# Column sums by token begun in the first expert stage, weight splits traced ahead and a double norm in two independent chains, in a two-block transformer kernel

## The chip, the cores and the metric

The kernel runs on one core of a Trainium2 chip. The time is the device time of one launch, in microseconds (us), from the start of the program to its end on that core. In the core, TensorE (PE in the profile; PEld is its weight loads) does the matmuls and writes to PSUM, VectorE (DVE) and ScalarE (ACT) read and write PSUM and SBUF, and SyncE (SP) issues the loads of the weights. Each engine works through its own list of instructions in the order in which they stand there, and semaphores tie the lists together.

## The reference

Everything is float32, with 256 tokens of 1024 features. A first block (two layers with FFNs) ends in a norm with a gain; a second block has two layers, each with two streams of tokens: x, the first block's output, and ctx.

```python
def rmsnorm(x, g):
    y = x * lax.rsqrt(jnp.mean(x * x, axis=-1, keepdims=True) + EPS)
    return y * g                                   # EPS = 1e-6
...
return rmsnorm(x, final_norm)                      # end of the first block
...
def rms_norm(x):
    return x * lax.rsqrt(jnp.mean(x * x, axis=-1, keepdims=True) + EPS)
def modulate_2(x, shift, scale):
    return rms_norm(x) * (1 + scale) + shift
```

In each layer of the second block a mixer takes `modulate_2` of both streams, and an expert layer (expert choice: 16 experts, each picks 32 tokens) follows and adds its result to them. In layer 0 x is thus normed twice in a row: with the gain of the first block's end, and again without one for the mixer. In layer 1 both streams are normed right after the expert layer of layer 0 has added its result.

## The kernel before

The streams stay in SBUF with features on partitions: `xT` and `xcT` are [128, 8, 256], feature k*128+p of token t at [p, k, t].

**Matmuls.** The second block's projections use three matmuls in a reduced float32 format for each product (`mm3`, L322 to L324): both operands are split into a high and a low part, and high*high, high*low and low*high are summed. A weight slice is split by ScalarE (`wsh`, L314) and VectorE (`wsl`, L315) into one of two buffers; an activation is split when it is made (`hh`, `hl`). So a split can begin only when TensorE has finished with the slice two before it.

**Weights.** SP loads weights in slots of 2 MB (`raw`, L294) that are handed round as a ring: a load waits until whatever was in its slot has been read. The loads that matter here: `ada` (the matrices of scale and shift), `wqk`, `wvf` and `wu` (projections of the mixer) and `sm` (small parameters, among them the one that `kr`, L1343, is multiplied by).

**A norm.** `sums` (L615 to L621): ScalarE squares a 128x256 slice, TensorE adds it over the partitions with a 128x32 weight of ones (L617), eight times; VectorE transposes in blocks of 32 (L619), and a small matmul (L621) leaves the 256 sums as a 128x8 column tile. `inv_sqrt` (L627, then L596 to L606) is ten small VectorE instructions; `spread` (L637, L639) copies and transposes the result to a row for each partition. `modulated` (L664 to L666) then makes the eight slices of `hh` and `hl`, with VectorE, ScalarE and VectorE in turn. For ctx in layer 1 its slices are queued (`later`) and given out between other work.

**The order of the work.** A string, `PLAN`, lists the stages of each layer's mixer (`x` norms a stream, `t` is the projection with `wqk`, `n` its small norms and transposes (L1337 to L1360), `v` that with `wvf`, `u` that with `wu`, `F` takes in loads of `ada` and adds their products, L473 and L479). The program is written in that order, and a scheduler then reorders the instructions of each engine by its own model of when each is ready.

**The double norm** of layer 0 (`st_x`, L1583 to L1592): with s1 the sum of squares of x and s2 that of gain*x, r1 = rsqrt(s1/n + EPS) and r2 = r1*rsqrt(r1*r1*s2/n + EPS). r2 is needed by the mixer's first norm, r1 only for the new x (L1592).

**End of the expert stage.** The last expert product of layer 0 (L1875) is weighted and split (L1884, L1885), put back by token by matmuls (L1888, L1889) and added to `xT` and `xcT` one slice at a time (L1891). Then comes the mixer of layer 1.

## Time and profile before

| | |
|---|---|
| median of three runs | 1552.39 us (1551.93 to 1553.54) |
| the profiled execution | 1550.65 us, of which its span is 1548.9 |
| TensorE busy | 1425.8 us, 92% of the span |
| TensorE weight loads busy | 990.0 us, 64% |
| VectorE, ScalarE busy | 894.8 us, 578.5 us |
| mean granted clock of TensorE | 0.975 of 2.4 GHz |

The profile shows one execution. The span runs from the first to the last instruction that it records; 1.75 us of the time lie around it. Times in rows are us from the span's start, "x8" counts instructions, "out<-in" are the program's names without buffer numbers, and brackets hold how long the engine sat idle before and what ended that. Ends of matmuls are modelled, so the distance between starts says more than a duration. A matmul in full float32 is recorded as two instructions.

In time the kernel is the first block (to 699), the mixer of layer 0 (its first norm and its `wqk`, `wu` and `wvf` projections lie in 699 to 750), its expert layer (to 1196), the mixer of layer 1, and the last expert layer (from about 1290 to the end).

### The profile page before, as it was taken

The page shows a single profiled execution, that of the slowest core. Times are in us where ns is not written, and L with a number is a line of the kernel's source. Part 1 is how long each engine was busy: PE and PEld are TensorE (multiplying, and loading weights), DVE is VectorE, ACT ScalarE, POOL GpSimd, SP SyncE. Part 2 cuts the span into 40 slices and gives each one's busy share as a digit, 9 for nine tenths or more (in the row PEclk, how much of TensorE's full clock was granted, in tenths as well). Part 3 has the DMA queues.
Part 4 walks back from the last instruction along what each step waited for, and adds up shares of the span by engine and source line. Part 5 has one row for each costly group of instructions (what it writes and reads, how often), then busy time and mean ns, then how long its engine had stood idle before and what let it go on. Part 6 is the DMA issues. An engine that isn't in the chain of part 4 may idle for free.

```text
span 1548.9 us, 25284 instructions
## 1 busy us (share of the span) xinstructions
PE 1425.8 (92%) x10360; PEld 990.0 (64%) x10362; DVE 894.8 (58%) x2051; ACT 578.5 (37%) x1180; POOL 5.0 (0%) x15
## 2 busy tenths in 40 slices
PE   5999999999999999999999999999998889897665
PEld 2965899997967999996754784443433656632111
DVE  5668788896776998966665542322224765422011
ACT  3455444443555444544654441211102564310000
POOL 0000000000000000000000000000000000000000
PEclk9999999999999999999999999999999999999788
DMA  9647678597424866554286976899993225699998
GB/s 396 261 178 297 261 275 323 216 394 302 179 110 162 313 259 233 210 210 171 113 315 252 404 305 251 329 414 388 415 368 162 110 109 198 276 428 428 427 427 341
DMA packets 33666, 434.09 MB, mean 280 GB/s; under 512 B 3728, under 2 KB 4368, under 8 KB 6032
## 3 DMA queue, kind: packets, MB, share of 16 engines
q1 hardware_dynamic: 32400, 429.92, 69.8%
q10 hardware_dynamic: 1152, 2.57, 0.5%
q8 instruction: 81, 1.33, 0.3%
q14 instruction: 33, 0.27, 0.0%
HBM read 431.43 MB, written 1.05 MB: 279 GB/s over the span
## 4 chain that ended last, share of the span: by engine, by line
PE 75%; DMA 10%; DVE 9%; ACT 2%; issue 1%; POOLq 0%; DVEq 0%; ACTq 0%; SPq 0%
PE g L322 13%; PE g L324 13%; PE g L323 13%; PE g L1838 7%; PE y L1875 5%; DMA raw<-in_md_dram 4%; PE t L473 3%; DMA raw<-in_mgu_dram 3%; DMA h<-in_mgu_dram 3%; DVE wsl L315 2%; PE m L1838 2%; PE t L1797 2%; PE y L1506 1%; PE g L1523 1%; PE y L1504 1%
## 5 line engine op out<-in xcount | busy, mean ns | idle before, releaser
L314 ACT ACTIVATE wsh<-raw 128x1024 fp32r<-128x1024 f32 (+4 forms) x236 | 242.8, 1033 | 316.4 <-PE g L323 233.9
L315 DVE TENSOR_TENSOR wsl<-raw,wsh 128x1024 fp32r<-128x1024 f32 (+4 forms) x236 | 279.5, 1188 | 88.9 <-ACT wsh L314 88.2
L322 PE MATMUL g<-h,wsh 128*128 128x256 f32 x1072 | 303.8, 286 | 3.7 <-ACT h L657 2.4
L324 PE MATMUL g<-h,wsl 128*128 128x256 f32 x1072 | 304.1, 285 | 2.0 <-DVE wsl L315 2.0
L323 PE MATMUL g<-h,wsh 128*128 128x256 f32 x1072 | 303.9, 285 | 0.2
L322 PEld LDWEIGHTS g<-h,wsh 128*128 128x128 f32 x1072 | 205.1, 192 | 9.5 <-ACT h L665 3.2
L324 PEld LDWEIGHTS g<-h,wsl 128*128 128x128 f32 x1072 | 205.6, 192 | 3.9 <-DVE wsl L315 2.8
L323 PEld LDWEIGHTS g<-h,wsh 128*128 128x128 f32 x1072 | 205.9, 192 | 1.4 <-DVE h L666 0.6
L1838 PE MATMUL g<-raw,xs 128*32 128x512 f32 x1232 | 165.2, 626 | 20.4 <-DMA raw<-in_mgu_dram 19.8
L1875 PE MATMUL y<-raw,a 128*32 128x512 f32 x736 | 99.9, 631 | 9.3 <-DMA raw<-in_md_dram 8.4
L1838 PEld LDWEIGHTS g<-raw,xs 128*32 128x32 f32 x1232 | 38.8, 112 | 106.6 <-issue 70.4
L324 PE MATMUL g<-gh,wsl 128*128 128x256 f32 x352 | 99.8, 284 | 1.5 <-DVE wsl L315 1.5
L322 PE MATMUL g<-gh,wsh 128*128 128x256 f32 x352 | 100.1, 284 | 0.0
L323 PE MATMUL g<-gl,wsh 128*128 128x256 f32 x352 | 99.8, 283 | 0.0
L438 DVE CUSTOM_DVE_ANT_0 raw<-raw,crowc,cols 128x1024 f32<-128x1024 f32 x64 | 80.7, 1280 | 1.2 <-DMA raw<-in_mod1t_dram 1.1
L473 PE MATMUL t<-raw,zc 128*32 128x512 f32 x512 | 71.4, 611 | 6.9 <-DMA raw<-in_mod_dram 6.9
L1802 ACT ACTIVATE xs<-t,modada,ra 128x128 f32<-128x128 f32 x32 | 14.6, 457 | 151.3 <-PE t L1797 107.7
L324 PEld LDWEIGHTS g<-gh,wsl 128*128 128x128 f32 x352 | 67.5, 192 | 1.9 <-DVE wsl L315 1.9
L322 PEld LDWEIGHTS g<-gh,wsh 128*128 128x128 f32 x352 | 67.5, 192 | 1.6 <-issue 1.2
L323 PEld LDWEIGHTS g<-gl,wsh 128*128 128x128 f32 x352 | 67.5, 192 | 0.8 <-issue 0.8
L1875 PEld LDWEIGHTS y<-raw,a 128*32 128x32 f32 x736 | 23.7, 113 | 64.3 <-issue 42.6
L1800 DVE TENSOR_SCALAR xs<-t,ra,modada 128x128 f32<-128x128 f32 x32 | 13.1, 410 | 87.6 <-PE t L1797 50.4
(480 smaller groups left out, 2327.3 us busy)
## 6 DMA issues: line engine op xcount, KB each, us to landing
raw<-in_mgu_dram SPq DMA_DIRECT2D x61, 2048.0 KB, 13.7
raw<-in_md_dram SPq DMA_DIRECT2D x28, 2048.0 KB, 12.0
raw<-in_ffgu_dram SPq DMA_DIRECT2D x22, 2048.0 KB, 8.9
raw<-in_ada_dram SPq DMA_DIRECT2D x19, 2048.0 KB, 7.8
raw<-in_mod_dram SPq DMA_DIRECT2D x12, 2048.0 KB, 9.5
raw<-in_mod1t_dram SPq DMA_DIRECT2D x11, 2048.0 KB, 9.7
raw<-in_ffd_dram SPq DMA_DIRECT2D x16, 1408.0 KB, 7.1
raw<-in_win_dram SPq DMA_DIRECT2D x6, 2048.0 KB, 12.6
```

The lines of the kernel that those rows point to most:

```text
L314: self.nc.scalar.activation(hi, src, AF.Copy)
L315: self.nc.vector.tensor_tensor(lo, src, hi.bitcast(F32), op=ALU.subtract)
L322: mm(out, ah, bh, start=first, stop=False)
L323: mm(out, ah, bl, start=False, stop=False)
L324: mm(out, al, bh, start=False, stop=last)
L438: nc.vector.tensor_tensor_reduce(junk, w[:, q, :], zr[:, i, :], 0.5, self.cols[:, o + 4 * s + q:o + 4 * s + q + 1], ALU.mult, ALU.add, m[: ...
L473: nc.tensor.matmul(acc[32 * j:32 * j + 32, :], zw[:, k, :], w[:, k, :], start=(k < 4), stop=(k >= 4))
L1504: nc.tensor.matmul(sc, self.qT[:, hd, ts], self.kT[:, hd, :nk], start=True, stop=False)
L1506: nc.tensor.matmul(sc, self.qrT[s2, hd // 2, ts], self.krT[s2, hd // 2, :nk], start=False, stop=True)
L1797: nc.tensor.matmul(ps, s["ht"][:, t, k * 128:(k + 1) * 128], oh[:, t, :], start=(t == 0), stop=(t == 1))
L1838: nc.tensor.matmul(banks[si][u][32 * e:32 * e + 32, :], xs[:, k, e * 32:e * 32 + 32], raw[:, u * 2048 + e * 512:u * 2048 + e * 512 + 512], ...
L1875: nc.tensor.matmul(ys[si][32 * e:32 * e + 32, :], hts[si][:, f * 128 + 32 * e:f * 128 + 32 * e + 32], raw[:, (fj * 4 + e) * 512:(fj * 4 + ...
```

## The change

There are three parts. **(1)** The norms of layer 1 begin inside the last write-back of the expert stage, for both streams: `sums2` squares each slice and multiplies it, as a 128x128 weight, with a selector of two columns, so that the sums come out with a token on each partition ([128, 2]), EPS included by one more matmul; `spread2` takes the rsqrt there and makes the row with two matmuls into PSUM. **(2)** The entry `E` at the front of layer 1's plan writes the first two weight splits of `wvf` ahead of the norm; `st_v` picks them up. **(3)** The double norm becomes two chains that don't depend on each other: with `gfin` = sqrt(gain*gain + EPS), made at the start of the kernel by thirteen small VectorE instructions, r2 = rsqrt(sum((x*gfin)^2)/n + EPS*EPS); r1's sum and rsqrt are written after it. The code of an option that was off (`EX`) goes away.

```diff
-PLAN = [..., '+U x0 x1 v0 u0 +H +Q F2 tj nj F1 ...']
+PLAN = [..., 'E +U x0 x1 v0 u0 +H +Q F2 tj nj F1 ...']
...
+    def sums2(self, x):
+        ps = self.ps(self.stag)[:, :2]
+        nk = x.shape[1]
+        nc.tensor.matmul(ps, self.ident, self.epsc, start=True, stop=False)
+        for k in range(nk):
+            sq = self.w([128, 256], "a256", NA2)
+            nc.scalar.activation(sq, x[:, k, :], AF.Square, scale=1.0 / 32)
+            for t in range(2):
+                nc.tensor.matmul(ps, sq[:, t * 128:t * 128 + 128], self.sel2[:, t, :], start=False, stop=(k == nk - 1 and t == 1))
+        return ps
+    def spread2(self, cp):
+        y = self.w([128, 2], "rsy2", 2)
+        self.rsqrt(y, cp, self.w([128, 2], "rst2", 2), self.w([128, 2], "rsc2", 2))
+        r = self.ps("y")[:, :256]
+        for t in range(2):
+            self.nc.tensor.matmul(r[:, t * 128:t * 128 + 128], y[:, t:t + 1].to_broadcast([128, 128]), self.ident, start=True, stop=True)
+        return r
...
-            w = self.split(raw[:, k0 * 512:(k0 + 2) * 512], 1024)
+            w = self.pre.pop(0) if self.pre else self.split(raw[:, k0 * 512:(k0 + 2) * 512], 1024)
...
         if si == 1:
             self.pump(len(self.vq))
-            self.h[1] = self.hc if l == 0 else self.modulated(xc, ..., later=VX > 0)
+            r = self.spread2(self.early.pop(1)) if l else None
+            self.h[1] = self.hc if l == 0 else self.modulated(xc, ..., r=r, later=VX > 0)
         elif l == 1:
-            r = (...) if EX else None
+            r = self.spread2(self.early.pop(0))
             self.h[0] = self.modulated(x, ..., r=r, pair=self.pair2())
         else:
-            y1 = self.inv_sqrt(self.sums(x), 1024)
-            s2 = self.sums(x, gain)
-            v = self.w([128, 8], "rsc2", 1)
-            nc.vector.tensor_tensor(v, y1, y1, op=ALU.mult)
-            nc.vector.tensor_tensor(v, v, s2, op=ALU.mult)
-            y2 = self.inv_sqrt(v, 1024)
-            nc.vector.tensor_tensor(y2, y2, y1, op=ALU.mult)
-            r2 = self.spread(y2)
+            r2 = self.spread(self.inv_sqrt(self.sums(x, self.gfin), 1024, EPS * EPS))
+            s1 = self.sums(x)
             a = self.scale_cols(mn, 1, "final_norm", 0)
             self.h[0] = self.modulated(x, a, mn, 0, 0, r=r2, pair=self.pair2())
-            r1 = self.spread(y1)
+            r1 = self.spread(self.inv_sqrt(s1, 1024))
...
+            elif c == "E":
+                self.pre = [self.split(self.raw("wvf")[:, i * 1024:i * 1024 + 1024], 1024) for i in range(2)]
...
-                    if EX and q == 3 and n == 1 and si == 0:
+                    if q == 3 and n == 1:
                         self.stag = ST[1]
-                        self.rx = ...
+                        self.early[si] = self.sums2(x)
```

With the new lines the line numbers shift. After the change the split stands at L313 and L314, `mm3` at L321 to L323, the products with `ada` at L490, `sums` at L654 to L660, `inv_sqrt` at L666, `spread` at L676 and L678, `modulated` at L703 to L705, the transposes of stage `n` at L1397, the write-back at L1927 and L1928.

VectorE, mixer of layer 0, the end of the norm. Before, the rsqrt of r1 (its last instruction is L606), then the second chain's transpose of its sums (L619), the product with r1 and the second rsqrt:

```order
L606 SCALAR_TENSOR_TENSOR rsy_7935<-rsc_7933,rsy_7935 128x8
L1583 TENSOR_TENSOR rsc_1233_7975<-rsy_7935 128x8
L619 STREAM_TRANSPOSE a_1231_7971<-y_7946 128x256
L1584 TENSOR_TENSOR rsc_1233_7975<-rsc_1233_7975,t_7973 128x8
L627 TENSOR_SCALAR rsc_7978<-rsc_1233_7975 128x8
```

After the change the chain of r2 (from `y_7927`) comes first and ends in its `spread` (L676, L678); L658 is the transpose of the other sums, those of r1 (`y_7973`), and L703 the first instruction of `modulated`:

```order
L623 SCALAR_TENSOR_TENSOR rsy_7958<-rsc_7956,rsy_7958 128x8
L676 COPY a_1228_7969<-rsy_7958 128x256
L678 STREAM_TRANSPOSE rsr_7971<-a_1228_7969 128x256
L658 STREAM_TRANSPOSE a_1239_7998<-y_7973 128x256
L703 SCALAR_TENSOR_TENSOR a_1244_8006<-xT_61,acol_8002,rsr_7971 128x256
L703 SCALAR_TENSOR_TENSOR a_1245_8010<-xT_61,acol_8002,rsr_7971 128x256
```

The second rsqrt has left the way to `modulated`, but the transpose that waits for the other sums still stands ahead of it.

TensorE, the same stage, where the ctx half of `wqk` ends (`g_8047` last) and the x half begins (`g_8048`). Before:

```order
L324 MATMUL g_8047<-wsh_8078,h_7145 128x448
L473 MATMUL t_8167<-raw_1268_8165,zc_1198_7872 32x512 x8
L473 MATMUL t_8179<-raw_1270_8177,zc_1198_7872 32x512
L322 MATMUL g_8048<-wsh_8050,hh_1240_7998 128x448
L323 MATMUL g_8048<-wsl_8051,hh_1240_7998 128x448
```

After; L656 is the last of the column sums of r1, `t_8186` the first product with `ada`:

```order
L656 MATMUL y_7973<-a_1238_7995,ones_68 32x256
L660 MATMUL t_8000<-a_1239_7998,cons_66 128x8
L490 MATMUL t_8186<-raw_1273_8184,zc_1204_7895 32x512
L321 MATMUL g_8067<-wsh_8069,hh_1242_8004 128x448
L322 MATMUL g_8067<-wsl_8070,hh_1242_8004 128x448
```

One product with `ada` stands here now, where nine stood. The others stand at the end of the stage (four in its middle). Before, the end of the `wqk` stage and the start of `wu` (`y_8294`):

```order
L323 MATMUL m_8049<-wsl_8135,hh_1240_7998 128x448
L324 MATMUL m_8049<-wsh_8134,hl_1241_7999 128x448
L473 MATMUL t_8179<-raw_1270_8177,zc_1198_7872 32x512 x3
L322 MATMUL y_8294<-h_7145,wsh_8290 128x256
L323 MATMUL y_8294<-h_7145,wsh_8290 128x256
```

After, the same place (`y_8313` is the start of `wu`):

```order
L322 MATMUL m_8068<-wsl_8154,hh_1242_8004 128x448
L323 MATMUL m_8068<-wsh_8153,hl_1243_8005 128x448
L490 MATMUL t_8186<-raw_1273_8184,zc_1204_7895 32x512 x3
L490 MATMUL t_8198<-raw_1275_8196,zc_1204_7895 32x512 x8
L1397 MATMUL t_8240<-cons_66,a_1287_8237 128x128 x2
L1397 MATMUL t_8251<-cons_66,a_1290_8248 128x128
L1397 MATMUL t_8240<-cons_66,a_1287_8237 128x128
L1397 MATMUL t_8251<-cons_66,a_1290_8248 128x128 x2
L1397 MATMUL t_8288<-cons_66,a_1301_8285 128x128
L1397 MATMUL t_8299<-cons_66,a_1304_8296 128x128
L321 MATMUL y_8313<-h_7168,wsh_8309 128x256
```

The last reads of both `ada` slots (`raw_1273`, `raw_1275`) now come after the whole `wqk` stage, and eight transposes of stage `n` stand ahead of `wu`.

VectorE, start of layer 1's mixer. Before, after the transpose of the sums two weight splits (L315) stand with the rsqrt, whose end is shown here:

```order
L604 SCALAR_TENSOR_TENSOR rsc_11877<-rsc_11877,rst_11880 128x8 x2
L606 SCALAR_TENSOR_TENSOR rsy_11879<-rsc_11877,rsy_11879 128x8
L637 COPY a_1980_11890<-rsy_11879 128x256
L639 STREAM_TRANSPOSE rsr_11892<-a_1980_11890 128x256
L664 SCALAR_TENSOR_TENSOR a_1982_11894<-xT_61,acol_11844,rsr_11892 128x256
```

After; `y_11819` and `y_11873` are the token sums of x and of ctx, `rsy_1991` and `rsy_2006` their rsqrt:

```order
L621 SCALAR_TENSOR_TENSOR rsc_1993_11943<-rsc_1993_11943,rst_1992_11942 128x2 x2
L613 TENSOR_SCALAR rsy_2006_11992<-y_11873 128x2
L623 SCALAR_TENSOR_TENSOR rsy_1991_11941<-rsc_1993_11943,rsy_1991_11941 128x2
L614 TENSOR_SCALAR rsy_2006_11992<-rsy_2006_11992 128x2
L616 TENSOR_TENSOR rst_2007_11993<-rsy_2006_11992 128x2
L617 TENSOR_TENSOR rst_2007_11993<-rst_2007_11993,y_11873 128x2
L314 TENSOR_TENSOR wsl_11931<-raw_1983_11928,wsh_11930 128x1024
L314 TENSOR_TENSOR wsl_11935<-raw_1983_11928,wsh_11934 128x1024
L703 SCALAR_TENSOR_TENSOR a_1998_11960<-xT_61,acol_11956,y_11953 128x256
```

The first instruction of ctx's rsqrt (L613) has come ahead of the last of x's, and both splits ahead of `modulated`. TensorE at the same place, after the change: the last write-backs (`t_11861` and the two after it are those of ctx) with the pairs of column sums (L635) between them:

```order
L635 MATMUL y_11819<-sel_7_72,a_1963_11845 128x2 x2
L1927 MATMUL t_11861<-a_1919_11586,a_1965_11853 128x256
L1928 MATMUL t_11861<-a_1919_11586,a_1966_11854 128x256
L635 MATMUL y_11819<-sel_7_72,a_1964_11849 128x2 x2
L1927 MATMUL t_11865<-a_1919_11586,a_1965_11853 128x256
L1928 MATMUL t_11865<-a_1919_11586,a_1966_11854 128x256
L635 MATMUL y_11873<-sel_7_72,a_1972_11875 128x2 x2
L1927 MATMUL t_11869<-a_1919_11586,a_1965_11853 128x256
```

After these, seven more pairs for `y_11873` and the two matmuls of x's `spread2` stand ahead of the mixer's first matmul. Before the change the eight sums of ctx stood further on, inside the `wvf` stage.

## Rows read from the trace of the kernel before

**Rows 1.** Windows: span, busy time by engine, granted clock, DMA share, GB/s.
```profile
1202.00:1208.00 6.00, 5.67 (x15) 3.95 (x16) 5.77 (x15) 4.17 (x12) 0.00 (x0) 0.63 0.02 4
...
1221.00:1233.00 12.00, 8.61 (x66) 7.98 (x65) 9.64 (x21) 6.99 (x18) 0.00 (x0) 1.00 0.71 282
...
1500.00:1549.00 49.00, 27.87 (x164) 6.84 (x160) 6.09 (x11) 1.19 (x2) 0.00 (x0) 0.85 0.85 358
```

**Rows 2.** Timeline of TensorE from layer 0's norm to the `wvf` stage: start, duration, instruction.
```profile
713.09 2.76 PE L473 MATMUL t<-raw,zc 128*32 128x512 f32 x18
716.33 0.47 PE L322 MATMUL g<-wsh,hh 128*128 128x448 f32 x1 [0.48 <-ACT hh L665]
...
732.59 1.06 PE L473 MATMUL t<-raw,zc 128*32 128x512 f32 x6
733.58 0.39 PE L322 MATMUL y<-h,wsh 128*128 128x256 f32 x1
...
744.21 0.50 PE L323 MATMUL g<-wsl,hh 128*128 128x512 f32 x1
```

**Rows 3.** Timeline of VectorE in the same norm.
```profile
710.92 0.45 DVE L619 STREAM_TRANSPOSE a<-y 128x256 f32<-128x256 f32 x1 [4.13 <-PE y L617]
...
715.25 1.28 DVE L664 SCALAR_TENSOR_TENSOR a<-xT,acol,rsr 128x256 f32<-128x256 f32 x3
...
723.16 1.04 DVE L315 TENSOR_TENSOR wsl<-raw,wsh 128x896 fp32r<-128x896 f32 x1
```

**Rows 4.** Timeline of SP's queue: two loads of this stretch.
```profile
715.07 0.33 SPq L294 DMA_DIRECT2D raw<-in_sm_dram  x1
724.23 0.33 SPq L294 DMA_DIRECT2D raw<-in_wu_dram  x1
```

**Rows 5.** DMA view of 690 to 746: size, us from issue to landing.
```profile
raw<-in_sm_dram SPq DMA_DIRECT2D x1, 2048.0 KB, 8.6
...
raw<-in_wu_dram SPq DMA_DIRECT2D x1, 1024.0 KB, 4.8
```

**Rows 6.** Timeline of VectorE at the start of layer 1's mixer.
```profile
1195.17 0.88 DVE L1891 SCALAR_TENSOR_TENSOR xcT<-t,modada,xcT 128x256 f32<-128x256 f32 x2 [0.50 <-PE t L1889]
...
1201.25 1.28 DVE L664 SCALAR_TENSOR_TENSOR a<-xT,acol,rsr 128x256 f32<-128x256 f32 x3
```

**Rows 7.** Timeline of TensorE there, to the end of the `wvf` stage.
```profile
1190.54 0.64 PE L617 MATMUL y<-a,ones 128*32 128x256 f32 x8
...
1202.34 0.80 PE L322 MATMUL g<-wsh,hh 128*128 128x512 f32 x1 [5.49 <-ACT hh L665]
...
1220.90 0.39 PE L324 MATMUL g<-wsh,hl 128*128 128x512 f32 x1
1221.12 0.28 PE L322 MATMUL y<-hh,wsh 128*128 128x256 f32 x1
```

**Rows 8.** Waits of SP's queue, 1236 to 1300: total, times, longest.
```profile
SPq L294 <- DVE a L1467: 44.2, 1, 44.2
```

**Rows 9.** Windows at the kernel's start; columns as in rows 1.
```profile
14.00:17.00 3.00, 0.11 (x4) 0.00 (x0) 3.00 (x13) 0.60 (x1) 0.00 (x0) 1.00 1.00 426
17.00:19.00 2.00, 1.91 (x16) 0.50 (x16) 1.76 (x11) 0.00 (x0) 0.00 (x0) 1.00 1.03 438
19.00:22.00 3.00, 0.02 (x3) 0.00 (x0) 0.84 (x2) 0.00 (x0) 0.00 (x0) 1.00 0.98 404
22.00:25.00 3.00, 2.77 (x16) 0.90 (x20) 0.00 (x0) 0.00 (x0) 0.00 (x0) 0.50 1.02 423
```

**Rows 10.** Timeline of TensorE: matmuls with a full float32 weight of 128x128.
```profile
944.18 0.71 PE L1797 MATMUL t<-a,h 128*128 128x128 f32 x4
944.73 0.61 PE L1797 MATMUL y<-a,h 128*128 128x128 f32 x4
...
1215.08 0.28 PE L621 MATMUL t<-a,cons 128*128 128x8 f32 x2
1215.22 0.71 PE L322 MATMUL g<-wsh,hh 128*128 128x512 f32 x2
```

More of the change, by code (lines that the diff above doesn't have):

```diff
@@ L34 @@
 VX = 1
-EX = 0
 AD = [int(c, 16) for c in 'A2220']
@@ L357, in setup @@
         nc.vector.memset(self.ones, 1.0)
+        self.epsc = self.t(c, [128, 2], F32, "epsc")
+        nc.vector.memset(self.epsc, EPS)
+        self.sel2 = self.t(c, [128, 2, 2], F32, "sel2")
+        nc.vector.memset(self.sel2, 0.0)
+        for t in range(2):
+            nc.vector.memset(self.sel2[:, t, t:t + 1], 1.0)
+        self.gfin = self.t(c, [128, 8], F32, "gfin")
         self.sel16 = self.t(c, [128, 32], F32, "sel16")
@@ L364, in setup @@
         self.pq, self.pf, self.pn, self.vc, self.pc, self.rowz = [], [], 0, 0, 0, {}
-        self.known = {}
+        self.known, self.early = {}, {}
         self.add_ring(3)
@@ L370, in setup @@
         self.stag = "t"
+        g = self.col("final_norm", 0, 8)
+        t = self.w([128, 8], "acol", 3)
+        nc.vector.tensor_tensor(self.gfin, g, g, op=ALU.mult)
+        nc.vector.tensor_scalar(self.gfin, self.gfin, EPS, None, op0=ALU.add)
+        c = self.w([128, 8], "acol", 3)
+        nc.vector.tensor_copy(c, self.gfin)
+        y = self.w([128, 8], "acol", 3)
+        self.rsqrt(y, c, t, c)
+        nc.vector.tensor_tensor(self.gfin, self.gfin, y, op=ALU.mult)
     def drop(self, *cms):
@@ L591, in scale_cols, with rsqrt @@
         return a
-    def rsqrt(self, y, c, t):
+    def rsqrt(self, y, c, t, u=None):
         nc = self.nc
@@ L606, in rsqrt @@
         nc.vector.scalar_tensor_tensor(y, c, 1.0, y, op0=ALU.add, op1=ALU.mult)
+    def sums2(self, x):
+        nc = self.nc
+        ps = self.ps(self.stag)[:, :2]
[11 more added lines that the diff above has]
+        r = self.ps("y")[:, :256]
+        for t in range(2):
+            self.nc.tensor.matmul(r[:, t * 128:t * 128 + 128], y[:, t:t + 1].to_broadcast([128, 128]), self.ident, start=True, stop=True)
+        return r
     def sums(self, x, gain=None):
@@ L622, in sums, with inv_sqrt @@
         return cp[:, :8]
-    def inv_sqrt(self, cp, n):
+    def inv_sqrt(self, cp, n, eps=EPS):
         nc = self.nc
         c = self.w([128, 8], "rsc", 2)
-        nc.vector.tensor_scalar(c, cp, 1.0 / n, EPS, op0=ALU.mult, op1=ALU.add)
+        nc.vector.tensor_scalar(c, cp, 1.0 / n, eps, op0=ALU.mult, op1=ALU.add)
         y = self.w([128, 8], "rsy", 3)
```

11 lines of the change are left out of this document (5 added, 6 removed).

## The prediction

> **What bounds the kernel now.** I read the windows first, to find where TensorE is not busy, then the timelines of TensorE, VectorE and SP at the two places that the change touches, and last the waits of SP's queue.
>
> TensorE is the bound of most of the kernel. In the norm of layer 0 it has work for the whole stretch: the nine products with `ada` (18 records from 713.09) cover all of its wait for `hh` but 0.48 us [rows 2]. VectorE has the waits there, 4.13 us for the second chain's sums [rows 3]. Whoever removes one of those waits gains only what TensorE waits, and whoever makes TensorE wait here loses it, since no slack follows.
>
> The start of layer 1's mixer is different. The last write-back ends at 1195.17 + 0.88 = 1196.05, `modulated` begins 5.2 us later [rows 6], and TensorE stands for 5.49 us; the `wvf` stage then takes from 1202.34 to 1221.12 [rows 7], the first six microseconds of it at a granted clock of 0.63, and in 1221 to 1233 TensorE is busy for 8.61 of 12 us [rows 1]. So this place has something to give.
>
> The end is bound by loads (DMA share 0.85, TensorE 27.87 of 49 [rows 1]). Whether a shift of the mixer reaches the end is told by SP's queue: the first load of the last experts waits 44.2 us for an instruction of the mixer, a VectorE one at L1467 [rows 8], so what the mixer gains or loses passes on.
>
> **Layer 0, the double norm.** The second chain's way from its sums to `modulated` was 710.92 to 715.25, 4.33 us [rows 3]. It would be gone if r2 could go on alone. But in VectorE's order the transpose of r1's sums stands ahead of the first `modulated`, and those sums now end as the last matmuls ahead of the x half, at about 713.1, where the ctx half ended [rows 2]. With the transpose's 0.45 [rows 3] `modulated` begins at 713.6 in place of 715.25: 1.65 us are won, and the x half starts at 714.7.
>
> Of the nine products one still stands in the wait. Eight go to the end of the `wqk` stage: 16 records at 2.76/18 = 0.153 us, 2.45 us [rows 2]. The stage itself ends at 732.59 - 1.65 = 730.9; three products (0.99, from the distance of two starts [rows 2]) follow until 731.9, then the eight until 734.4. If that were all, `wu` would begin 0.8 us late (before at 733.58).
>
> It is not all, because slots are handed round. `ada`'s slots are now free only at 731.9 and 734.4, so three loads change places: `sm` takes the slot of `wqk`, and waits for its fourth split, 723.16 + 1.04 - 1.65 = 722.6 in place of 715.07 [rows 3, 4]; it lands 8.6 us later [rows 5], at 731.2, and holds up `kr`, which stands on VectorE ahead of the second rsqrt of stage `n`. `wu` takes the slot of the first `ada` and is issued at 731.9 in place of 724.23 [rows 4]; with its 4.8 us [rows 5] it lands at 736.7. The split on ScalarE comes after that, about 1.0 us (the VectorE half of one took 1.04 [rows 3]), and stands behind stage `n`'s copies, which wait for the late rsqrt: `wu`'s matmuls begin at about 738.1. `wvf` is issued at 734.4; at `sm`'s 8.6 it lands at 743.0, while `wu` is still computed.
>
> The `wu` stage lasted 733.58 to 744.21, 10.6 us [rows 2], eight transposes within. These now stand ahead of it, in the wait; at the nearest price, 0.55 for four records of a 128x128 weight [rows 10], they were 1.1 us of it. So the next stage begins at 738.1 + 9.5 = 747.6 in place of 744.21: **+3.4 us**. Low bound +2.5 (ScalarE's queue adds nothing: 737.7, and a `modulated` that starts 0.5 sooner); high bound +5.5, below.
>
> **The clock.** TensorE would stand from 734.4 to 738.1 with only transposes. After 3 us of waiting the granted clock was still 1.00 once (14 to 17, then 17 to 19) and 0.50 once (19 to 22, then 22 to 25) [rows 9]; six microseconds at 0.63 after 5.49 us of waiting cost 0.37 x 6 = 2.2 us [rows 1, 7]. I count no fall in layer 0, and a half in layer 1. The Trainium skill, page TensorE: Matmul & The Clock Gate, section on oscillation in real kernels, says that gaps in the matmul stream send the array back to its half clock, so that the next burst starts cold. Rows 9 agree in one case of two. By that rule layer 0 would pay 1.5 to 2.2 us more, and the sum would be about +0.4 instead of -1.5.
>
> **Layer 1, sums in the write-back.** The trace has no matmul with a full 128x128 weight and two columns. One with eight columns took 0.14 from its start to the next [rows 10]; one with 128 columns 0.55/2 = 0.275 [rows 10]. I take 0.22, nearer to the second, since there too each matmul loads its own weight. The first group is ten matmuls (eight sums and two of EPS), 2.2 us, in place of 0.64 [rows 7]: +1.55. Then a pair stands ahead of each of five write-backs, where three groups stood. What such an interlude costs, changing over included, I work out from the `wvf` stage: 1221.12 - 1202.34 = 18.8 us hold 48 matmuls at 1221.12 - 1220.90 = 0.22 to 0.23 [rows 7], 10.9 us, and 2.2 us of slow clock; the remaining 5.7 are eight sums of ctx, 0.71 each. Three at 0.71 become five at 0.75: +1.6. The write-backs end 3.2 us later, at 1199.25.
>
> Ctx's last square, its pair and the hand-over take another 1.3 us (estimated from two instructions of about 0.4 and their waits), to 1200.55. VectorE then has the first instruction of ctx's rsqrt, and only behind it the last of x's; five such instructions are 1.0 us. The two splits, 1.2 us each (an estimate from 1.04 for 896 columns [rows 3], for 1024), stand ahead of `modulated`, which begins at 1203.95 in place of 1201.25 [rows 6]. So the norm is **later**, by 2.7 us, though its sums began sooner.
>
> What is won is behind it. TensorE starts 1.1 us after `modulated` (1202.34 against 1201.25 [rows 6, 7]), at 1205.05. The stage is now 10.9 us without sums of ctx; I add 1.3 for a third split that waits behind `modulated` on VectorE, or for the rest of a slow clock. It ends at 1217.25 in place of 1221.12: -3.9. Of the 3.4 us of idle time in 1221 to 1233 [rows 1] I give back 1.0, since ctx's chain no longer competes there with splits. **-4.9 us.** Bounds: at 0.275 a matmul, 1.1 more; with the whole slow clock 0.9 more, with a second late split 1.0 more, and nothing given back 1.0: -0.9. At 0.14, 1.6 less, no added 1.3 and a little more given back: -8.
>
> **The start.** `gfin` is 13 small VectorE instructions, 2.2 us at the 0.17 of their kind (17 to 19: 1.76 us for 11 [rows 9]). TensorE waits there for loads (DMA share near 1.0 in 14 to 25 [rows 9]), which hide it; without that cover it would be 2.2 us. The removed products of the second rsqrt lay in VectorE's waiting time. Both: 0.
>
> **Sum.** +3.4 - 4.9 = -1.5 us: 1550.65 of the profiled execution becomes 1549.1. That execution is 1.74 below the median of 1552.39; from the median, 1550.9.
>
> **The rivals.**
> - *Slower: layer 1 gives nothing back.* Its norm waits for ctx's sums and both splits. If a matmul costs 0.275, the clock falls whole and the idle time stays, the gain is 0.9 and the sum +2.5, 1554.9; with layer 0 at its upper end +4.6, 1557.0. It decides by more than 0.2% (3.1 us, about what a measurement of this kernel can tell from no change) when the first `modulated` of layer 1 begins later than about 1207. For it: VectorE's order. Against: ctx's 5.7 us are taken off in any case. 0.18.
> - *The clock falls in layer 0 too*: the sum +0.4, 1552.8. For it rows 9's second case, against it the first. 0.13.
> - *Faster: layer 0 loses nothing.* Loads land sooner than 8.6 and 4.8 in a quieter queue, or the transposes and the `ada` products fill the wait. Then only the 0.8 us of moved products are late, less the 1.1 of transposes that go into the wait: about 0, and layer 1 gives -4.9 or more: 1547.5, down to 1544.4. Against it: `wu`'s slot is free only at 731.9, whatever the queue. 0.22.
> - *No effect*: both places lose and win less than 1 us, 1552.4. 0.05.
> - The forecast keeps 0.42, its own range 1548.5 to 1553.5.
>
> **How the numbers follow.** The range leaves out the far ends of the slower and the faster rival, about 0.1 at each side: 1545.5 to 1556. Faster by over 0.2%: most of the faster rival (0.20) and a third of the forecast (0.14): 0.34. Slower by over 0.2%: two thirds of the slower rival (0.12), a third of the clock's (0.04) and a little of the forecast: 0.18. Within: 0.48.
>
> **What the profile after would show.** Right: `modulated` of layer 0 at about 713.6; `wu` issued near 732 and TensorE idle for 3 us ahead of its first matmul; the next stage at 747.6. In layer 1, write-backs that end near 1202.6 (3.4 late from layer 0, 3.2 by themselves), `modulated` at 1207.4, a `wvf` stage of 12 us without sums, the `wu` stage at 1220.7. Wrong: `wu`'s matmuls in layer 0 at 733 or so (then the slots did not matter); column sums that cost 0.4 us a matmul; or an idle stretch in layer 1 that moves from ahead of the `wvf` stage into it, so that it still ends at 1221 plus what layer 0 lost.

## The result, and the profile after

The changed kernel takes **1563.81 us** (median of five runs, 1562.81 to 1567.59) where the kernel before, run beside it, takes 1552.39 (1550.68 to 1553.71): a ratio of 1.0077, interval 1.0063 to 1.009. It is slower by 11.4 us, above the range. The profiled execution took 1563.81, its span is 1562.0, the mean granted clock 0.970.

Where the time went is read from SP's queue, whose loads follow the work that frees their slots. First four loads of the kernel before (start, duration, instruction): the first `ada` load of layer 0's mixer, the first `md` load of its expert layer, `wqk` of layer 1, and the first load after layer 1's mixer.

```profile
692.88 0.33 SPq L294 DMA_DIRECT2D raw<-in_ada_dram  x1
...
918.44 0.43 SPq L294 DMA_DIRECT2D raw<-in_md_dram  x1
...
1161.21 0.33 SPq L294 DMA_DIRECT2D raw<-in_wqk_dram  x1
...
1289.29 18.55 SPq L294 DMA_DIRECT2D raw<-in_mgu_dram  x4
```

The same loads after the change, with `sm` and `wu` of layer 0 between them:

```profile
693.29 0.33 SPq L293 DMA_DIRECT2D raw<-in_ada_dram  x1
...
722.34 0.33 SPq L293 DMA_DIRECT2D raw<-in_sm_dram  x1
732.32 0.33 SPq L293 DMA_DIRECT2D raw<-in_wu_dram  x1
...
924.52 0.43 SPq L293 DMA_DIRECT2D raw<-in_md_dram  x1
...
1167.78 0.33 SPq L293 DMA_DIRECT2D raw<-in_wqk_dram  x1
...
1304.94 0.33 SPq L293 DMA_DIRECT2D raw<-in_mgu_dram  x1
```

The queue is 0.41 us late ahead of layer 0's mixer, 6.08 behind it, 6.57 ahead of layer 1's mixer and 15.65 behind it. So layer 0 costs 5.7 us, layer 1 9.1, and the end gives about 2.5 back (span 13.1 longer). Below, "shifts +5.7/+9.1" stands for these two differences: from `ada` to `md`, and from `wqk` to the load after the mixer, each against before. They come from one execution each (the first is -0.2 to -0.4 in the kernels whose layer 0 is unchanged); the verdicts rest on the medians.

**Layer 0.** TensorE from the last products with `ada` to `wvf`, in answer to [rows 2]:

```profile
731.21 2.78 PE L490 MATMUL t<-raw,zc 128*32 128x512 f32 x22
...
734.85 0.44 PE L1397 MATMUL t<-cons,a 128*128 128x128 f32 x2 [0.55 <-ACT cq L1399]
...
739.29 0.51 PE L321 MATMUL y<-h,wsh 128*128 128x256 f32 x1 [0.62 <-ACT wsh L313]
...
749.79 0.40 PE L321 MATMUL g<-wsh,hh 128*128 128x512 f32 x1
```

Before the change, the first `wvf` product of layer 0 stands ahead of the one in [rows 2]:

```profile
743.52 0.63 PE L322 MATMUL g<-wsh,hh 128*128 128x512 f32 x2
```

VectorE in the norm, in answer to [rows 3]:

```profile
713.26 0.45 DVE L658 STREAM_TRANSPOSE a<-y 128x256 f32<-128x256 f32 x1 [5.26 <-PE y L656]
713.63 1.24 DVE L703 SCALAR_TENSOR_TENSOR a<-xT,acol,rsr 128x256 f32<-128x256 f32 x3
```

Windows (columns as in [rows 1]):

```profile
736.00:739.00 3.00, 1.20 (x4) 0.44 (x4) 0.00 (x0) 2.94 (x8) 0.00 (x0) 1.00 1.05 407
739.00:742.00 3.00, 2.61 (x11) 2.32 (x12) 2.36 (x2) 1.18 (x2) 0.00 (x0) 0.56 0.83 350
742.00:745.00 3.00, 3.00 (x24) 3.00 (x24) 0.12 (x1) 0.38 (x1) 0.00 (x0) 0.87 0.78 235
```

`modulated` begins earlier, as forecast; `wu` is issued 8.1 us later than before [rows 4], TensorE stands in six pieces, 3.0 us in all, ahead of its first matmul, and then runs at a lower clock until about 743.

**Layer 1.** TensorE, in answer to [rows 7]; L635 are the sums by token, two records for each matmul:

```profile
1197.16 1.93 PE L635 MATMUL y<-sel,a 128*128 128x2 f32 x16
...
1199.49 0.50 PE L635 MATMUL y<-sel,a 128*128 128x2 f32 x4
1199.86 0.37 PE L1927 MATMUL t<-a,a 128*128 128x256 f32 x1
...
1201.44 0.85 PE L635 MATMUL y<-sel,a 128*128 128x2 f32 x4
1202.15 0.56 PE L1927 MATMUL t<-a,a 128*128 128x256 f32 x1
...
1205.28 5.97 PE L635 MATMUL y<-sel,a 128*128 128x2 f32 x28
...
1215.40 0.79 PE L321 MATMUL g<-wsh,hh 128*128 128x512 f32 x1 [2.61 <-ACT hh L704]
...
1224.98 0.50 PE L322 MATMUL g<-wsl,hh 128*128 128x512 f32 x1 [0.94 <-DVE wsl L314]
...
1230.61 0.28 PE L321 MATMUL y<-hh,wsh 128*128 128x256 f32 x1
...
1249.30 0.53 PE L322 MATMUL g<-wsl,h 128*128 128x192 f32 x1 [3.95 <-DVE wsl L314]
```

VectorE, in answer to [rows 6] (L1930 is the write-back's addition):

```profile
1205.52 0.48 DVE L1930 SCALAR_TENSOR_TENSOR xcT<-t,modada,xcT 128x256 f32<-128x256 f32 x1 [0.80 <-PE t L1928]
...
1211.28 0.16 DVE L613 TENSOR_SCALAR rsy<-y 128x2 int32<-128x2 int32 x1 [3.83 <-PE y L635]
1211.36 0.15 DVE L623 SCALAR_TENSOR_TENSOR rsy<-rsc,rsy 128x2 f32<-128x2 f32 x1
...
1214.33 1.26 DVE L703 SCALAR_TENSOR_TENSOR a<-xT,acol,y 128x256 f32<-128x256 f32 x3
...
1247.76 0.48 DVE L703 SCALAR_TENSOR_TENSOR a<-xcT,acol,y 128x256 f32<-128x256 f32 x1
1248.15 1.09 DVE L314 TENSOR_TENSOR wsl<-raw,wsh 128x896 fp32r<-128x896 f32 x1
```

Windows, first the last write-backs of the kernel before:

```profile
1192.00:1198.00 6.00, 3.75 (x20) 1.95 (x19) 4.57 (x10) 2.93 (x5) 0.00 (x0) 1.00 0.00 0
```

After the change:

```profile
1194.00:1200.00 6.00, 5.72 (x49) 4.00 (x42) 2.70 (x7) 2.18 (x4) 0.39 (x1) 1.00 0.13 44
1200.00:1206.00 6.00, 6.00 (x31) 6.00 (x31) 2.60 (x7) 3.42 (x9) 0.00 (x0) 0.52 0.01 3
1206.00:1212.00 6.00, 5.68 (x27) 5.60 (x28) 1.86 (x14) 2.31 (x3) 0.00 (x0) 0.50 0.00 0
...
1248.00:1254.00 6.00, 4.70 (x17) 4.45 (x18) 2.64 (x4) 0.51 (x1) 0.00 (x0) 0.50 0.00 0
```

Three things matter here. A record of the sums takes 0.12 us in the first group and 0.21 in the last; in between, the granted clock goes to half while TensorE is recorded busy for 6.00 of 6.00 us (the longest gap in the records ahead of that is 0.28 us, at 1196.67). VectorE waits 3.83 us for ctx's sums, with the last instruction of x's rsqrt (L623) behind that wait. And at 1249 TensorE waits 3.95 us for a `wsl` that stands on VectorE behind a slice of ctx, and the clock falls again.

### The profile page after: what moved, and what is told of

It reads as the page before. It is cut to its first block, busy times and chain, and to the rows that moved or that the text cites. A ratio compares the mean times of both kernels' runs of the same rounds, so it can differ in the third digit from the quotient of the medians.

```text
span 1562.0 us, 25376 instructions
## 1 busy us (share of the span) xinstructions
PE 1437.6 (92%) x10402; PEld 1005.4 (64%) x10402; DVE 895.1 (57%) x2057; ACT 580.6 (37%) x1180; POOL 5.0 (0%) x15
## 4 chain that ended last, share of the span: by engine, by line
PE 76%; DMA 9%; DVE 8%; ACT 3%; issue 1%; ACTq 0%; DVEq 0%; SPq 0%
PE g L323 13%; PE g L322 13%; PE g L321 13%; PE g L1877 7%; PE y L1914 5%; DMA raw<-in_md_dram 4%; PE t L490 3%; DMA raw<-in_mgu_dram 3%; DMA h<-in_mgu_dram 3%; PE m L1877 2%; DVE wsl L314 2%; PE t L1836 2%; PE y L1545 1%; PE g L1562 1%; PE y L1543 1%
## 5 line engine op out<-in xcount | busy, mean ns | idle before, releaser
L313 ACT ACTIVATE wsh<-raw 128x1024 fp32r<-128x1024 f32 (+4 forms) x236 | 242.6, 1032 | 319.8 <-PE g L322 229.4
L314 DVE TENSOR_TENSOR wsl<-raw,wsh 128x1024 fp32r<-128x1024 f32 (+4 forms) x236 | 279.8, 1190 | 95.7 <-ACT wsh L313 94.7
L321 PE MATMUL g<-h,wsh 128*128 128x256 f32 x1072 | 303.9, 286 | 3.7 <-ACT h L696 2.4
L323 PE MATMUL g<-h,wsl 128*128 128x256 f32 x1072 | 304.3, 285 | 1.9 <-DVE wsl L314 1.9
L321 PEld LDWEIGHTS g<-h,wsh 128*128 128x128 f32 x1072 | 205.2, 192 | 9.5 <-ACT h L704 3.2
L323 PEld LDWEIGHTS g<-h,wsl 128*128 128x128 f32 x1072 | 205.7, 192 | 3.7 <-DVE wsl L314 2.7
L323 PE MATMUL g<-gh,wsl 128*128 128x256 f32 x352 | 99.9, 284 | 1.7 <-DVE wsl L314 1.7
L321 PE MATMUL g<-gh,wsh 128*128 128x256 f32 x352 | 100.1, 284 | 0.0
L490 PE MATMUL t<-raw,zc 128*32 128x512 f32 x512 | 73.3, 627 | 5.1 <-DMA raw<-in_mod_dram 5.1
L323 PEld LDWEIGHTS g<-gh,wsl 128*128 128x128 f32 x352 | 67.5, 192 | 2.3 <-DVE wsl L314 2.3
L321 PEld LDWEIGHTS g<-gh,wsh 128*128 128x128 f32 x352 | 67.5, 192 | 1.6 <-issue 1.2
L1839 DVE TENSOR_SCALAR xs<-t,ra,modada 128x128 f32<-128x128 f32 x32 | 13.1, 410 | 87.6 <-PE t L1836 49.4
```

The source lines that it names most:

```text
L313: self.nc.scalar.activation(hi, src, AF.Copy)
L314: self.nc.vector.tensor_tensor(lo, src, hi.bitcast(F32), op=ALU.subtract)
L321: mm(out, ah, bh, start=first, stop=False)
L323: mm(out, al, bh, start=False, stop=last)
L490: nc.tensor.matmul(acc[32 * j:32 * j + 32, :], zw[:, k, :], w[:, k, :], start=(k < 4), stop=(k >= 4))
```

## The experiments

Eighteen kernels ran. Theory A: the narrow sums bring the clock down. Theory B: the place of the norm and the order that the scheduler makes of it, whatever the clock. Theory C: the late slot of `wu` is the whole loss in layer 0.

**1. The parts apart.** `double_norm_alone` has part (3) only:

```diff
-'E +U x0 x1 v0 u0 ...
+'+U x0 x1 v0 u0 ...
...
-r = self.spread2(self.early.pop(0))
+r = None
...
-if q == 3 and n == 1:
+if False:
```

> Only part 3 is kept (the double norm as two chains); layer 1's mixer begins as before the change. In the changed kernel SP's queue was 0.41 us late before layer 0's norm and 6.08 us late after it. If the loss of layer 0 is part 3's own, through the slots that are freed late, this kernel is 5 to 6.5 us slower than the kernel before, with wu issued near 732 and a granted clock under 1.00 in 736 to 742. The rival, that the loss at layer 0 came from what else is in the program (a later start, other buffers), gives less than 2 us.

1556.93 us against 1552.63, ratio 1.0023 (1.0013 to 1.0032), shifts +5.8/+1.4. By its median it loses 4.3 us, a little under the range. Layer 0's loss comes from part (3) and needs nothing of the others.

`early_sums_alone` has parts (1) and (2), with the double norm as before:

```diff
-r2 = self.spread(self.inv_sqrt(self.sums(x, self.gfin), 1024, EPS * EPS))
-s1 = self.sums(x)
+y1 = self.inv_sqrt(self.sums(x), 1024)
+s2 = self.sums(x, gain)
...
+r2 = self.spread(y2)
...
-r1 = self.spread(self.inv_sqrt(s1, 1024))
+r1 = self.spread(y1)
```

> Only parts 1 and 2 are kept (sums by token in the write-back, splits traced ahead); the double norm is as before the change. SP's queue lost another 9.5 us between 1171 and 1305 in the changed kernel, of which 3 were given back later. First theory, the column sums with two columns bring the clock down while TensorE is busy with them: 6 to 9 us slower than before, granted clock at 0.50 from the write-back on. If the parts add up without touching each other, this run and double_norm_alone together make about 11.4 to 13 us. The rival, that layer 1 lost only because it was reached with the slots and loads of a late layer 0: under 3 us.

1555.91 (ten runs, 1554.82 to 1562.98), 1.0025 (1.0013 to 1.0038), shifts -0.4/+12.3. Slower, and in layer 1 alone, but by its median 3.3 us: between the 6 to 9 of the one theory and the "under 3" of the other. The profiled execution is the longest of the ten; eight lie between 1554.8 and 1556.8, so the +12.3 is likely too large for the usual one. The two parts sum to 7.6 us and the whole change costs 11.4: they don't add.

**2. What in the early sums costs time.** `early_old_sums`: as `early_sums_alone`, but the sums that begin early are the old ones (a 32-column weight of ones, 256 moving columns). The same two lines change for ctx, with `pop(1)`.

```diff
-self.early[si] = self.sums2(x)
+self.early[si] = self.sums(x)
-r = self.spread2(self.early.pop(0))
+r = self.spread(self.inv_sqrt(self.early.pop(0), 1024))
```

> As early_sums_alone, but the sums in the write-back are the old ones (weight of ones with 32 columns, 256 columns moving, VectorE transpose, spread by VectorE), begun at the same place for both streams, with the splits ahead. First theory (narrow matmuls cost the clock): the granted clock stays at 1.00 through the write-back and the sums, the write-backs end about 3 us sooner than in early_sums_alone, and the time is 4 to 9 us under early_sums_alone, at or below the kernel before. The rival (the order on VectorE, with ctx's sums and both splits ahead of the first norm, costs the time): as slow as early_sums_alone within 3 us, at a clock of 1.00.

1546.27, 0.9956 (0.9942 to 0.9971), shifts -0.3/-4.4. The clock is 1.00 through the write-back and the sums, and falls behind them, where TensorE waits for the norm:

```profile
1196.00:1202.00 6.00, 4.73 (x24) 2.06 (x24) 4.51 (x9) 3.49 (x7) 0.00 (x0) 1.00 0.02 4
1202.00:1208.00 6.00, 2.46 (x7) 2.00 (x8) 5.74 (x28) 1.56 (x4) 0.00 (x0) 0.69 0.00 0
```

`wide_selector`: the narrow sums again, but the selector's two columns are repeated 64 times each, so that 128 columns move through the same weight.

```diff
-ps = self.ps(self.stag)[:, :2]
+pf = self.ps(self.stag)[:, :128]
+ps = pf.rearrange("p (t j) -> p t j", j=64)
...
-nc.tensor.matmul(ps, self.ident, self.epsc, start=True, stop=False)
+nc.tensor.matmul(ps, self.ident, self.epsc.unsqueeze(2).to_broadcast([128, 2, 64]), start=True, stop=False)
...
-    nc.tensor.matmul(ps, ..., self.sel2[:, t, :], ...)
+    nc.tensor.matmul(ps, ..., self.sel2[:, t, :].unsqueeze(2).to_broadcast([128, 2, 64]), ...)
-return ps
+return ps[:, :, 0]
```

> As early_sums_alone, but each sum by token has 128 moving columns in place of two (the selector's two columns repeated 64 times; the result is the same and the weights are too). More work for TensorE in each matmul. First theory: the clock stays at 1.00, or falls later, so that a matmul costs at most the 0.275 us of a 128-column one in place of 0.43, and the kernel is 2 to 6 us faster than early_sums_alone though its matmuls are longer. The rival (the loading of 128x128 weights in full float32 sets the pace, and the clock falls for the wait alone): 0 to 3 us slower than early_sums_alone, the clock at 0.50 as there.

1548.04, 0.9969 (0.9956 to 0.9981), shifts -0.2/-0.25: 64 times the columns, and 7.9 us less than `early_sums_alone`. Its TensorE timeline and two windows:

```profile
1195.36 3.06 PE L636 MATMUL y<-sel,a 128*128 128x128 f32 x26
...
1201.23 0.50 PE L321 MATMUL g<-wsh,hh 128*128 128x512 f32 x1 [1.12 <-ACT hh L705]
...
1232.43 0.53 PE L322 MATMUL g<-wsl,h 128*128 128x192 f32 x1 [3.96 <-DVE wsl L314]
```

```profile
1190.00:1196.00 6.00, 6.00 (x55) 6.00 (x55) 3.68 (x10) 5.18 (x12) 0.00 (x0) 1.00 0.10 36
1196.00:1202.00 6.00, 3.87 (x29) 3.42 (x28) 5.59 (x23) 2.30 (x6) 0.00 (x0) 1.00 0.01 1
```

TensorE and its weight loads are as busy as in the changed kernel's 1200:1206, but the clock stays at 1.00; a record takes 0.12 us (3.06 for 26), as with two columns at full clock. Theory A holds for the clock. Theory B may have a share of the time: with the wide form the scheduler no longer puts ctx's first instruction ahead of x's last, so the 7.9 us hold clock and order together. And the 3.96 us wait is still there.

**3. E.** The plan entry taken out, once with narrow and once with old sums:

```diff
-'E +U x0 x1 v0 u0 ...
+'+U x0 x1 v0 u0 ...
```

> As early_sums_alone (3.3 us slower than before by its median, 10.4 in its profiled execution), without the two splits traced ahead. With the old sums the splits ahead were worth 3.7 us. If they help here too, 6 to 8 us slower than before; if what matters is the clock that the narrow sums bring down, within 2 us of early_sums_alone, and its granted clock at 0.50 through the sums.

1558.53, 1.0038 (1.0025 to 1.0051), shifts -0.4/+11.8: 2.6 us more than with E by the medians, but the two intervals overlap.

> As early_old_sums (6.4 us faster than before), without the two splits traced ahead. Before the change the scheduler had moved x's sums into the write-back by itself, and put the two splits between them and the rsqrt. If the gain comes from ctx's sums having left the wvf stage, it stays: 5 to 7 us faster than before. If it comes from the splits, 0 to 2 us faster.

1549.6, 0.9985 (0.9975 to 0.9995), shifts -0.3/-1.5: 3.3 us more than `early_old_sums`, and between the two ranges expected. Part (2) gains about three microseconds with the old sums; with the narrow ones as much is likely, but not shown.

**4. The slot of `wu`.** In layer 0 `wu` gets a buffer of its own (8 KB a partition) in place of a slot of the ring, so it needn't wait for `ada` (the plan also opens and closes the pool of that buffer):

```diff
+if nm == "wu" and self.l == 0:
+    s = self.t(self.wux, [128, 2048], F32, "raww", 1)
+    self.nc.sync.dma_start(s, src)
+    self.raws[nm, i] = s
+else:
     self.raws[nm, i] = self.slot(src)
```

With part (3) alone:

> As double_norm_alone (4.3 us slower than before), but wu of layer 0 is loaded into a buffer of its own, so its load need not wait for the slot of the first ada load. The order of the products with ada (eight at the end of the wqk stage) stays. If the late slot is the cause, wu is issued right behind sm, near 723, its matmuls follow the wqk stage with less than 1 us of idle time, the clock stays at 1.00 there, and the time comes to -1.7 to +0.8 us against before. The rival (kr, the late rsqrt of stage n and the transposes hold up wu's split on ScalarE whatever the load does): +3 to +5 us as without the buffer.

1550.37, 0.9988 (0.9978 to 0.9998), shifts -0.2/0.0, where `double_norm_alone` had 1556.93 and +5.8. In this stretch (705 to 751) TensorE has one idle piece left, and the clock is 1.00:

```profile
711.81 0.39 PE L660 MATMUL t<-a,cons 128*128 128x8 f32 x2 [0.54 <-DVE a L658]
```

With the whole change; here, and in the last kernel of 8, `spread2` also shares the small tiles of the old rsqrt in place of its own:

> The changed kernel with wu of layer 0 in its own buffer; narrow sums and ctx's order stay. double_norm_wu_apart was 6.2 us under double_norm_alone: 1556.5 to 1558.5. If what layer 1 loses depends on how layer 0 ends: 1559 or more, or under 1556.

1556.97 (ten runs, 1554.84 to 1562.42), 1.0035 (1.0022 to 1.0049), shifts -0.2/+8.8: 6.8 us less than the changed kernel, with layer 0's loss gone and layer 1's still there. And the buffer in the kernel before, as a control:

> Control: the kernel before the change with wu of layer 0 in its own buffer and nothing else. TensorE had no wait there (0.48 us in the norm), so -0.5 to +0.5 us against before.

1555.3 against 1552.3, 1.002 (1.001 to 1.003), shifts +2.1/+1.9, a miss. So the buffer is not free where the slot was early anyway: 3.0 us with no idle piece above 0.5 us in layer 0's stretch. What costs them I did not find. Theory C stands in spite of it: with the buffer, part (3) has no shift left in layer 0.

**5. The wait at 1249.** `VX` says how many of ctx's queued slices are given out at a time; 4 puts them ahead of the splits.

```diff
-VX = 1
+VX = 4
```

> As wide_selector (4.6 us faster than before), with ctx's slices of modulated given out four at a time in place of one (VX = 4), so that all eight stand on VectorE ahead of the wu splits. In wide_selector, in early_sums_alone and in the changed kernel alike TensorE waits 3.95 us for the low half of the second wqk split, which stands behind ctx's last slices on VectorE, and its clock falls after that. If that order is the third loss, the wait is gone, the clock stays at 1.00 through 1226 to 1238, and the time is 4 to 6.5 us under wide_selector: 1541.5 to 1544. The rival (the slices cost the same wherever they stand, the wait moves into the wvf and wu stages): within 1.5 us of wide_selector.

1542.67 (1540.27 to 1543.36) against 1553.36, 0.9929 (0.9915 to 0.9944), shifts -0.4/-5.2: 5.4 us less than `wide_selector`. The largest idle pieces of TensorE between 1202 and 1262 are now

```profile
1215.46 0.39 PE L321 MATMUL y<-hh,wsh 128*128 128x256 f32 x1 [1.42 <-ACT wsh L313]
1224.29 0.44 PE L321 MATMUL g<-wsh,hh 128*128 128x448 f32 x1 [1.21 <-DVE vv L770]
```

and the clock is 1.00 from 1190 to 1256. The same edit on the changed kernel:

> The changed kernel with ctx's slices given out four at a time, nothing else; the narrow sums stay. If the 3.95 us wait for the second wqk split and the fall of the clock behind it are a loss of their own: 5 to 7 us under the changed kernel, 1557 to 1559, with the clock at 0.50 through the sums as before. If they only follow from the late start: within 2 us of 1563.8.

1562.04, 1.006 (1.0042 to 1.0078), shifts +5.5/+5.1: only 1.8 us less than the change, a miss. The wait of 3.95 is gone, and two new ones stand in the `wu` stage:

```profile
1234.23 0.35 PE L321 MATMUL y<-hh,wsh 128*128 128x256 f32 x1 [2.01 <-DVE a L703]
...
1236.98 0.58 PE L323 MATMUL y<-hh,wsl 128*128 128x256 f32 x1 [2.27 <-DVE wsl L314]
```

**6. The sums of the changed kernel mended.** Wide, and wide with `VX = 4`:

> The changed kernel with 128 moving columns in its sums by token, nothing else. Additive by parts: layer 0's loss stays (4.3), layer 1 as in wide_selector (-4.6): 1552 to 1555, 9 to 12 us under the changed kernel. If the three parts together lose something of their own (11.4 against 4.3 and 3.3): 1556 or more.

1557.15, 1.0029 (1.0016 to 1.0042), shifts +7.0/+1.4: 6.7 us less than the change, and in layer 1. It misses the additive 1552 to 1555: with the clock of the sums mended, too, the parts lose more together than apart.

> The changed kernel with both: only layer 0's late slots are left. 1542.7 (wide_selector_ctx_early) plus the 4.3 to 6 us of the double norm: 1546.5 to 1549. If the double norm's loss comes back later, 1543 to 1545.

1551.4 (ten runs, 1549.62 to 1558.0), 1.0002 (0.9988 to 1.0017), shifts +6.6/-3.7: another 5.8 us, and level with the kernel before, but above the 1546.5 to 1549 expected.

**7. The clock by itself.** `changed_x_only` begins only x's sums early (17 narrow matmuls with that of EPS, in place of 34):

```diff
-if q == 3 and n == 1:
+if q == 3 and n == 1 and si == 0:
-r = self.spread2(self.early.pop(1)) if l else None
+r = None
```

> The changed kernel with sums by token in the write-back for x alone (two columns, as there); ctx is summed in the wvf stage with the old sums. Layer 0 stays as it is. x's rsqrt now waits for nothing of ctx, and 16 of the 34 narrow matmuls are gone. If the run of 14 narrow matmuls for ctx with nothing between them is what holds the clock down and the norm back: layer 1's first norm begins about 5 us sooner against the end of the write-back, the clock is 1.00 through the write-back, and the time is 4 to 8 us under the changed kernel's 1563.8. If ctx's sums are worth as much in the wvf stage as they cost here: within 3 us of it.

1560.27, 1.0046 (1.0028 to 1.0063), shifts +6.9/+3.8: 3.5 us less than the change, between the two ranges, and a miss on the clock. Half of the narrow matmuls are enough for its fall, and ctx's early sums have no part in it:

```profile
1196.00:1202.00 6.00, 5.72 (x40) 4.89 (x34) 3.20 (x8) 2.48 (x5) 0.39 (x1) 0.82 0.12 44
1202.00:1208.00 6.00, 3.90 (x18) 3.60 (x17) 3.53 (x9) 2.31 (x3) 0.00 (x0) 0.50 0.00 0
```

`changed_filler` keeps the changed kernel whole and adds sixteen matmuls with 256 columns, one for each squared slice, whose result nobody reads:

```diff
+pf = self.ps("t")
 for k in range(nk):
     ...
+    nc.tensor.matmul(pf[:32, :256], self.ones[:, :32], sq, start=True, stop=True)
```

> The changed kernel with 16 matmuls more: each slice's square is also multiplied by the 128x32 weight of ones (256 columns moving), and the result is read by nobody. It adds about 0.2 us of TensorE to each, 3.5 us in all, among the narrow sums; the scheduler's order shifts a little with it. Theory of the clock: the granted clock stays at 1.00 through the write-back, a narrow instruction takes 0.11 us from start to start in place of 0.21, and the kernel is 1 to 5 us faster than 1563.8 though it does more. Rival (the time is that of the weight loads and of the order): 2 to 5 us slower, the clock at 0.50 as before.

1570.78 (1565.19 to 1578.0), 1.0115 (1.0079 to 1.0152), shifts +6.6/+8.7. In the traced execution a hit on the clock but for 0.50 in 1201 to 1204; a miss on the time. Its windows, and a group of narrow sums:

```profile
1202.00:1208.00 6.00, 6.00 (x26) 2.98 (x26) 1.49 (x2) 3.42 (x8) 0.00 (x0) 0.83 0.01 3
1208.00:1214.00 6.00, 6.00 (x43) 4.73 (x43) 3.12 (x7) 3.03 (x6) 0.00 (x0) 1.00 0.00 0
```

```profile
1209.68 1.84 PE L636 MATMUL y<-sel,a 128*128 128x2 f32 x16
```

The narrow records are back at 0.115 us: their half speed was the clock's, nothing else's. But the kernel is 7.0 us slower than the changed one. Its trace is the fastest of four executions; the others ran at a lower mean clock (0.963 to 0.971, against 0.973), so what costs the time, the filler's work or a clock that falls elsewhere, is not shown.

**8. The parts put together.** All parts with old sums and `wu` apart; the same with `VX = 4`; and all parts with wide sums, `VX = 4` and `wu` apart. The edits are those above.

> All three parts, with the old column sums in the place of those by token and wu of layer 0 in its own buffer. If the two causes are the ones named (the clock under the narrow sums, the slot of wu), their sum is that of early_old_sums (-6.4) and of double_norm_wu_apart (-1.7 to +0.8): 1544.5 to 1547. The rival, a further loss that belongs to the parts together (the changed kernel lost 11.4 us where its parts alone lost 4.3 and 3.3): 1548 or more.

1543.77, 0.9946 (0.993 to 0.9961), shifts -0.2/-1.6: a little under the range, and nothing of a further loss by the parts together.

> As all_old_sums_wu_apart (1543.8), with ctx's slices given out four at a time. With the old sums TensorE waited 2.44 us for a wqk split behind ctx's slices. If the order is to blame there too: 1.5 to 3.5 us faster than 1543.8; if not, within 1.5 us of it.

1551.06, 0.998 (0.9971 to 0.9989), shifts -0.1/+0.1. A miss: the same edit that gains 5.4 us with wide sums costs 7.3 with the old ones. Its TensorE waits 3.17 us for a split of `wu` that stands behind ctx's slices:

```profile
1222.76 0.58 PE L323 MATMUL y<-hh,wsl 128*128 128x256 f32 x1 [3.17 <-DVE wsl L314]
```

> All three parts of the change, with 128 moving columns in the sums by token, ctx's slices given out four at a time, and wu of layer 0 in its own buffer. If the three causes (clock under the narrow sums, order of ctx's slices, slot of wu) are separate, the gains add: wide_selector_ctx_early's 8 to 11 us under before and the 1.9 of double_norm_wu_apart: 1539.5 to 1542.5. If they share one wait, no faster than 1543.8, which all_old_sums_wu_apart took.

1542.55, 0.9939 (0.9922 to 0.9957), shifts -0.1/-6.7. No better than `wide_selector_ctx_early`, which leaves the double norm and the slot alone. Elsewhere part (3) with the buffer gained a little: 1.9 us by itself (`double_norm_wu_apart`), 2.5 with the old sums (overlapping intervals).

## Why the prediction was wrong

**The start** (`gfin`) was put at 0. The queue is 0.41 us late ahead of layer 0's mixer, but one trace can't tell that from nothing: in the traces of the other kernels, which all make `gfin`, the same load stands between 2.1 us earlier and 3.2 later than before.

**Layer 0**: the steps were right, the size was small. First `modulated` at 713.6 (measured 713.63), `sm` issued at 722.6 (722.34), `wu` at 731.9 (732.32), its first matmul at 738.1 (739.29). One row was misread: 744.21 in [rows 2] is the second `wvf` product, the first stands at 743.52. So the `wu` stage lasted 9.9 us, not 10.6, and the next stage was due at 746.9; the term, +3.4, is the same. It came at 749.79, less the 0.41 of the start 2.5 later than due. Of these, 0.8 were there at `wu`'s first matmul. The other 1.7 are the clock: the stage was counted at 8.8 without a fall and lasted 10.5, its first fourteen matmuls taking 3.5 us (to 742.83) where 0.12 each make 1.7. This is the rival "the clock falls in layer 0 too", which I gave 0.13. The term was +3.4, the layer cost 4.3 us by the median of `double_norm_alone` and 5.5 to 7.0 in the traces of the kernels with part (3) and the ring's slot. The cause, `wu`'s slot, is shown: a buffer for `wu` alone takes 6.6 to 6.8 us away.

**Layer 1** is where the prediction failed. It was to give 4.9 us and cost 9.1: of the 14.0 between them, 3.8 lie ahead of the `wvf` stage, 3.0 in it and 7.2 behind it.

The first step that failed is "Layer 1, sums in the write-back". Its price of 0.22 us a matmul was right at full clock (two records of 0.12). But it counted one pair of ctx behind the last write-back, "its pair", where the order shown with the change has seven; six pairs, 2.6 us at its own price, are missing from the sum. And it lacked that these matmuls don't keep the clock: I had looked for a fall only where TensorE waits; it fell where it was busy. The seven pairs took 5.97 us; 28 records of 0.12 would be 3.3. That the write-backs still ended as forecast (1206.0 less the 6.57 of shift: 1199.4, forecast 1199.25) is luck: a pair between them was put at 0.75, took 0.37 where the clock was still high (1199.49 to 1199.86), and 0.71 only because the clock had halved (1201.44 to 1202.15). Ctx's last sums, forecast to be complete at 1200.55, ended at 1211.25 less 6.57, 1204.7. "VectorE then has the first instruction of ctx's rsqrt, and only behind it the last of x's" was read rightly, and so the delay passed on whole: TensorE began 6.5 us later than before (1208.8 against 1202.34 [rows 7]) where 2.7 were forecast.

The `wvf` stage was to last 12.2 us and lasted 15.2: its first twelve matmuls stand 0.44 apart in place of 0.23 (1215.40 to 1220.68), 2.5 us, and 0.94 went to the third split. So it ended 2.9 us later than before, forecast 3.9 earlier.

The second step that failed is the last term, "I give back 1.0": it had the wrong sign, and is the largest part of the miss. From the end of that stage to the load behind the mixer the changed kernel takes 74.3 us where the kernel before takes 68.2. For the same 290 records TensorE is idle for 13.3 us in place of 10.3, and busy for 61.0 in place of 57.9. The wait of 3.95 us for `wsl` is more than the added idle time (a wait of 1.72 us before, in the `wu` stage, is gone, as the term hoped), and the half clock behind it makes 2.3 us of 4.70 busy ones. I had looked at ctx's chain as something that leaves the `wvf` stage, and not at where its slices would stand instead. Experiments 5 and 6 show this term with wide sums, 5.4 and 5.8 us.

**The rivals.** "Layer 1 gives nothing back" was the right side, for another reason than its own (0.275 a matmul, a fall after a wait), and ended at 1557.0; the measured time lies beyond it because none of the cases had the six pairs or a clock that falls during the sums. The point that I named, a first `modulated` later than about 1207, was passed: 1214.33 less 6.57 is 1207.8.

The idea of the early norm was sound: with sums in which the clock stays up, it gains 6.4 us (`early_old_sums`, though there the clock falls behind them) or, with ctx's slices put right, 10.7 (`wide_selector_ctx_early`), the best version together with `all_wide_ctx_early`.

**Open.** How much of the 6.7 to 7.9 us between narrow and wide is clock and how much the order that the scheduler then chooses: `changed_filler` separates the clock but brings work of its own. Why the parts don't add, with wide sums either. Executions of one kernel differ by as much as a part is worth: `early_sums_alone` ran at about 1556 or at 1560 to 1563, `changed_wu_apart` at 1555 to 1558 or at 1561 to 1562, and all five of the changed kernel took over 1562. The mean clock goes with it at least once (in `changed_wide_ctx_early` 0.971 and 0.972 in the three longest, 0.975 to 0.978 in the others); what decides it no run tells. And the 3.0 us of the control.
